# A streaming-encoder trunk on one Trainium2 core: the steps of a Strassen-like feed-forward put in one fixed order, engine by engine

## The chip, the core and the metric

The kernel runs on one core of one Trainium2 chip. The core has TensorE for matrix products (PE in the profile, PEld its loads of the stationary operand), VectorE (DVE), ScalarE (ACT), GpSimd (POOL) and SyncE, whose queue (SP) issues the DMAs here. Each engine works through its own instructions in the order in which they stand in the program, and waits on semaphores for the others.

The metric is the time of the program on the device, in microseconds (us), lower is better. It is taken over several runs; one further run is profiled, and all times of single instructions come from that one.

## What is computed

Two layers act on x of shape (1, 512, 1024) in float32. Layer 0 mixes by pooling, layer 1 by chunked attention with 16 heads; each is followed by a gated feed-forward of width 2816. The change touches the feed-forward of both layers and nothing else:

```python
def conv_ffn(h, w_gate, w_val, conv_w, conv_b, w_out):
    S = h.shape[1]
    a = h @ w_gate
    ap = jnp.pad(a, ((0, 0), (CONV_W - 1, 0), (0, 0)))
    a = ap[:, 0:S] * conv_w[0] + ap[:, 1:S + 1] * conv_w[1] + ap[:, 2:S + 2] * conv_w[2] + conv_b
    return (jax.nn.silu(a) * (h @ w_val)) @ w_out

def reference(x, ...):
    for i in range(DEPTH):
        h = rmsnorm(x, mix_norm[i])
        ...
        h = rmsnorm(x, ffn_norm[i])
        x = x + conv_ffn(h, ffn_w_gate[i], ffn_w_val[i], ffn_conv_w[i], ffn_conv_b[i], ffn_w_out[i])
    return x
```

## The kernel before

**Tiles.** The width of 2816 is cut into 22 tiles of 128, called f = 0 to 21. The frames stand along the free dimension (512), channels along the partitions. Every float32 operand of a product is held as two parts: a high part (the value rounded to the format that TensorE takes) made by ScalarE with a copy, and a low part (value minus high part) made by VectorE. A product is high x high, high x low and low x high, all summed in one bank of PSUM.

**Kinds of tiles** (`KIND`, L53). Tiles 0 and 1 are made early, 2 to 4 in the plain way, tile 5 by `apart`, tiles 6 to 21 by `strassen` (L581). Tiles 8 to 21 are "wide": a product's high and low moving parts go through TensorE as one matmul of 512 columns.

**One Strassen tile.** Gate and value weights of the tile are treated as a 2 x 2 block problem that takes seven products instead of eight. In the order of TensorE they are b11, b21, t2, t3, t1, b22, t4. A wide product is four matmuls of 512 columns (L601) and four of 256 (L603). The products b11, t2, t1 and b22 add up in one bank (`st_m`), b21 has its own (`st_b`), t3 and t4 share a third (`st_t`). The steps around them, with the short names used below (a number in brackets is the line):

- s1 to s4 (L631, L632, L638, L639), VectorE: sums and differences of the raw weights, into the tiles `sb` and `sa`; s2 needs s1, s4 needs s2.
- h1, h2, h3 (L406, ScalarE, 1024 wide) and l1, l2, l3 (L407, VectorE): high and low parts of the gate weights, of `sa` and of `sb`. h4, l4 (L99, L100, 512 wide): those of the value weights' last block. b11 and b21 need h1 and l1, t2 and t3 need h2 and l2, t1 and b22 need h3 and l3, t4 needs h4 and l4.
- a1 (L607, ScalarE) copies b11 out of PSUM, v1 t2, x1 t1, a3 (L669) b22. Since these four products share a bank, t2 waits for a1, t1 for v1, and b22 for x1.
- a2 and x2 (L613, VectorE) add b21 and t3; a5, v2, x3 (L619) and a4 (L671) fold the two halves of a bank together; v3 and v4 (L679) add t4.
- c0 (L418, ScalarE), c1 and c2 (L421, VectorE) are the convolution, c3 (L422, ScalarE) the SiLU, c4 (L672, VectorE) the product with the value, c5 (L99, ScalarE) and c6 (L100, VectorE) the high and low part of the result, which the output product reads.

**Places.** `tour` (L707) interleaves neighbouring tiles: while tile f is made, tile f-1 (o) is finished and tile f+1 (n) is begun. Each round of a tile has seven places, 0 to 6; on TensorE they are b11 of f, b22 of o, b21 of f, t4 of o, t2 of f, t3 of f, t1 of f. A table of letters says whose next steps are issued at a place:

```python
for k, who in enumerate(("of", "fo", "of", "fon", "of", "fon", "nf")):
```

**Output products.** The 22 tiles go to the output in four groups (`OUT`, L55: 5, 6, 6 and 5 tiles). While group g+1 is made, the output of group g (`output`, L684) is worked off behind the places: after each product some three or four matmuls of it follow, so that they are spread over the group. For each of the eight output tiles d there is one load of weights `wo_r` (its buffer is single), a high part `ow_h` (ScalarE) and a low part `ow_l` (VectorE), 15 or 18 matmuls, and an addition to X (L703, VectorE) that waits for the last of them. The spreading begins some places after the group before is complete (L58, used at L759):

```python
WAIT, HOLD = 2, 3
```

**What sets the order.** TensorE's order is written out by hand everywhere in the feed-forward. From tile 8 on (`ORDERED`, L54) VectorE's and ScalarE's are too: they run what is issued at a place in the order of the code. For earlier tiles a scheduler orders these two. SyncE's queue holds the loads in the order in which they are asked for, each waiting until its buffer is free.

Of the kernel before, what the change touches and what calls it, by code (L numbers as in the profile page):

```python
# [17 lines left out]
F32 = mybir.dt.float32  # L18
F32R = mybir.dt.float32r
# [4 lines left out]
P = 128  # L24
S = 512
# [44 lines left out]
def trunk(ctx: ExitStack, tc: tile.TileContext, xt, xT, cols, band, edge, poolw, gv, wout, wqk, wv, wo, rel, out):  # L70
# [307 lines left out]
    def ffn(l, first, pool, acc, summed=None):  # L378
# [35 lines left out]
        def hidden(f, a, finish):  # L414

            cw = [col[:, C_CW[l] + 4 * f + j:C_CW[l] + 4 * f + j + 1] for j in range(4)]
            c = g_tile(f"c{f}")
            nc.scalar.activation(c, a, AF.Identity, scale=cw[2], bias=cw[3])  # L418
            yield
            for j in range(1, 3):  # L420
                nc.vector.scalar_tensor_tensor(c[:, j:], a[:, :S - j], cw[2 - j], c[:, j:], op0=OP.mult, op1=OP.add)  # L421
# [159 lines left out]
        def strassen(f):  # L581

            wide = f in WIDE
            g, v = (raw_tile(f"gv{l}_{f}_{i}", gv[l, f, i]) for i in range(2))
            yield

# [3 lines left out]
            def product(o, hl, z, name, first):  # L590


# [9 lines left out]
                for i, c in enumerate(cs):  # L602
                    nc.tensor.matmul(o[:, 0], lo[:, c], B[i, name][:, 0], start=False, stop=i == 3, **how)  # L603

            def copy(x, o):
# [14 lines left out]

            def flat(o):
                return o.rearrange("p c n -> p (c n)")


            *w1, lo = parts(g, 1024, f"g1_{f}", later=True)
            yield
            lo()
            yield
            sa, sb = (sum_tile(f"s{x}{f}") for x in "ab")
            a11, a12, a21, a22, s2, s3, s1, s4 = (x[:, z * S:(z + 1) * S] for x in (g, v, sa, sb) for z in range(2))  # L630
            nc.vector.tensor_add(s1, a21, a22)  # L631
            nc.vector.tensor_sub(s2, s1, a11)  # L632
            main, side = bank("S", "m"), bank("P", "b")
            product(main, w1, 0, "b11", True)
            yield
            a = pool.tile([P, S], F32, name=f"a{f}", tag="a", bufs=2)
            copy(a, main)
            nc.vector.tensor_sub(s3, a11, a21)  # L638
            nc.vector.tensor_sub(s4, a12, s2)  # L639
            *w2, lo = parts(sa, 1024, f"g2_{f}", later=True)  # L640
            yield
            lo()
            product(side, w1, 1, "b21", True)
            yield
            add(a, side)
            fold(a[:, :HALF], a)
            *w3, lo = parts(sb, 1024, f"g3_{f}", later=True)
            yield
            lo()
            product(main, w2, 0, "t2", False)  # L650
            yield
# [5 lines left out]
            yield  # L657
            w4 = [tmp.tile([P, S], F32R, name=f"g4_{f}_{c}", tag="g", bufs=6) for c in "hl"]
            split(a22, *w4)
            product(main, w3, 0, "t1", False)  # L660
            yield
            x = g_tile(f"w{f}") if wide else val[:, HALF:]
            copy(x, main)
            add(x, side)
            fold(val[:, HALF:], x)
            yield
            product(main, w3, 1, "b22", False)
            yield
            nc.scalar.activation(a[:, HALF:], main[:, 0], AF.Copy)  # L669
            if wide:  # L670
                nc.vector.tensor_add(a[:, HALF:], a[:, HALF:], main[:, 1])  # L671
            gate = hidden(f, a, lambda c: nc.vector.tensor_mul(c, val, c))  # L672
            next(gate)
            yield
            next(gate)
            product(side, w4, 0, "t4", False)
            yield
            for c in range(2 if wide else 1):
                nc.vector.tensor_add(val[:, :HALF], val[:, :HALF], side[:, c])  # L679
            yield  # L680
            run(gate)
            yield

        def output(g):  # L684
# [22 lines left out]
        def tour():  # L707

            for f in range(NF):
                if KIND[f] == "p":  # L710
                    yield from plain(f)
                elif KIND[f] == "s" and KIND[f - 1] == "p":
                    old, new = None, strassen(f + 1)
                    for j, _ in enumerate(apart(f)):
                        if j in (3, 5, 6):
                            next(new)
                        yield
                elif KIND[f] == "s":
                    now, new = new, strassen(f + 1) if f + 1 < NF else None
                    for k, who in enumerate(("of", "fo", "of", "fon", "of", "fon", "nf")):  # L720
                        if f == ORDERED and k == 0:
                            order.enter_context(tc.manual_schedule(engines={ET.DVE, ET.Activation}))
                        for x in who:
                            if step := {"o": old, "f": now, "n": new}[x]:
                                next(step)
                        if old or k not in (1, 3):
                            yield
                    old = now
            for k in range(6):
                next(old)  # L730
                if k in (1, 3):
                    yield
            order.close()

        with tc.manual_schedule(engines={mybir.EngineType.PE}):
# [13 lines left out]
            for g, (b, m) in enumerate(OUT):  # L749
# [3 lines left out]
                for at in range(1, points + 1):  # L753
# [350 lines left out]
```

## Time and profile before

| what | value |
|---|---|
| time, 3 runs | median 1029.67 us (1029.55 to 1029.67) |
| the profiled run's own time | 1029.36 us |
| its span, first to last instruction | 1027.6 us |
| granted TensorE clock, mean over the span | 0.993 |
| DMA | 102.82 MB, mean 100 GB/s |

The rows of the profile read so: start and length in us, engine, line, operation, output <- inputs, shape, count; in square brackets how long the engine stood idle just before and which instruction released it. Groups of instructions show the busy time, the mean length in ns, and the idle time before them with its releaser. A busy TensorE is not TensorE at its peak, since a matmul's length overlaps with the next one's: 0.39 us long, they start every 0.23 us.

### The profile page before, as it was taken

The numbers are of one execution on the slowest core, as the hardware profiler recorded it, in microseconds if no ns is written. First come the engines' busy times: TensorE is split into PE (matmuls) and PEld (weight loads), VectorE is DVE, ScalarE is ACT, GpSimd is POOL, SyncE is SP. The second block draws the span as 40 slices with busy tenths as digits, with TensorE's granted clock in tenths as the row PEclk, the third lists the DMA queues.
The fourth block names the chain that finished last, engine by engine and source line by source line (L and its number), as shares of the span: only waits on it lengthen the run. The fifth ranks groups of instructions, "written<-read, shape, count | busy, mean of one in ns | idle before, by whom it ended". The sixth has DMA issues, their size and how long they took to land.

```text
span 1027.6 us, 13793 instructions
## 1 busy us (share of the span) xinstructions
PE 983.9 (96%) x5038; PEld 818.3 (80%) x5038; DVE 823.2 (80%) x1452; ACT 570.7 (56%) x990; POOL 103.2 (10%) x90
## 2 busy tenths in 40 slices
PE   9999999899999899999999999999999899988998
PEld 8788987787877688888888787888987677776776
DVE  8999888888888855452677888999888888888853
ACT  7665555454554445344898987565554545454431
POOL 2200000000000004103535441000000000000000
PEclk9999999999989999999999999999999999999999
DMA  8322323232323224323343242322332233222223
GB/s 324 97 82 84 104 88 97 82 102 89 98 73 113 57 67 146 103 86 108 115 124 98 84 122 73 112 92 88 103 105 78 92 92 93 92 92 93 63 75 114
DMA packets 37427, 102.82 MB, mean 100 GB/s; under 512 B 4432, under 2 KB 7904, under 8 KB 37360
## 3 DMA queue, kind: packets, MB, share of 16 engines
q1 hardware_dynamic: 37296, 101.90, 31.3%
q8 instruction: 40, 0.66, 0.2%
q14 instruction: 27, 0.22, 0.1%
q0 software_dynamic: 32, 0.04, 0.0%
q10 hardware_dynamic: 32, 0.00, 0.0%
HBM read 95.60 MB, written 2.14 MB: 95 GB/s over the span
## 4 chain that ended last, share of the span: by engine, by line
PE 49%; DVE 37%; ACT 10%; issue 3%; DMA 0%; DVEq 0%; ACTq 0%
DVE g_l L407 8%; ACT g_h L406 5%; DVE c L421 4%; PE out L121 4%; PE out L122 4%; PE out L120 4%; DVE ow_l L100 3%; PE gv L121 3%; PE qk L121 3%; PE qk L120 3%; PE qk L122 3%; PE gv L122 3%; PE gv L120 3%; DVE v L679 2%; DVE v L619 2%
## 5 line engine op out<-in xcount | busy, mean ns | idle before, releaser
L601 PE MATMUL st_m<-two,g_h 128*128 128x512 f32 x224 | 74.7, 415 | 20.5 <-ACT g_h L406 14.9
L121 PE MATMUL out<-one,ow_h 128*128 128x512 f32 x224 | 88.3, 394 | 0.0
L122 PE MATMUL out<-one,ow_l 128*128 128x512 f32 x224 | 88.3, 394 | 0.0
L120 PE MATMUL out<-one,ow_h 128*128 128x512 f32 x224 | 88.2, 394 | 0.0
L99 ACT ACTIVATE ow_h<-wo_r 128x640 fp32r<-128x640 f32 (+1 forms) x64 | 50.2, 784 | 43.8 <-PE out L121 35.7
L406 ACT ACTIVATE g_h<-sa 128x1024 fp32r<-128x1024 f32 x32 | 34.0, 1061 | 72.1 <-DVE sa L638 65.2
L601 PEld LDWEIGHTS st_m<-two,g_h 128*128 128x128 f32 x224 | 40.4, 192 | 40.4 <-ACT g_h L406 25.3
L703 DVE TENSOR_TENSOR X<-out,X 128x512 f32<-128x512 f32 (+1 forms) x65 | 44.0, 678 | 35.6 <-PE out L122 35.6
L601 PE MATMUL st_m<-h,g_h 128*128 128x512 f32 x224 | 70.3, 395 | 0.0
L603 PEld LDWEIGHTS st_m<-two,g_l 128*128 128x128 f32 x224 | 40.1, 190 | 34.8 <-DVE g_l L407 28.2
L100 DVE TENSOR_TENSOR ow_l<-wo_r,ow_h 128x640 fp32r<-128x640 f32 (+1 forms) x64 | 56.7, 885 | 14.0 <-ACT ow_h L99 14.0
L603 PE MATMUL st_m<-two,g_l 128*128 128x256 f32 x224 | 48.2, 298 | 14.8 <-DVE g_l L407 13.7
L422 ACT ACTIVATE c<-c 128x512 f32<-128x512 f32 x44 | 27.6, 630 | 58.8 <-DVE c L421 58.7
L421 DVE SCALAR_TENSOR_TENSOR c<-a,col,c 128x511 f32<-128x511 f32 (+1 forms) x76 | 56.6, 747 | 2.8 <-ACT c L418 1.8
L122 PE MATMUL qk<-wqk_h,two 128*128 128x512 f32 x128 | 51.4, 402 | 0.0
L120 PE MATMUL qk<-wqk_h,two 128*128 128x512 f32 x128 | 50.8, 409 | 0.0
L601 PEld LDWEIGHTS st_m<-h,g_h 128*128 128x128 f32 x224 | 42.9, 192 | 9.9
L121 PE MATMUL qk<-wqk_l,two 128*128 128x512 f32 x128 | 50.8, 397 | 0.0
L122 PEld LDWEIGHTS out<-one,ow_l 128*128 128x128 f32 x224 | 42.6, 190 | 6.5
L120 PEld LDWEIGHTS out<-one,ow_h 128*128 128x128 f32 x224 | 42.5, 190 | 6.2
L99 ACT ACTIVATE one<-c 128x512 fp32r<-128x512 f32 x28 | 17.6, 629 | 53.0 <-DVE c L672 51.8
L121 PEld LDWEIGHTS out<-one,ow_h 128*128 128x128 f32 x224 | 42.6, 190 | 5.3
(375 smaller groups left out, 2998.3 us busy)
## 6 DMA issues: line engine op xcount, KB each, us to landing
gv_r<-gv SPq DMA_DIRECT2D x86, 512.0 KB, 3.4
wo_r<-wout SPq DMA_DIRECT2D x32, 384.0 KB, 3.1
wo_r<-wout SPq DMA_DIRECT2D x32, 320.0 KB, 2.9
wqk_r<-wqk SPq DMA_DIRECT2D x16, 512.0 KB, 3.5
wv_r<-wv SPq DMA_DIRECT2D x8, 512.0 KB, 3.4
wo_r<-wo SPq DMA_DIRECT2D x8, 512.0 KB, 3.4
xt<-xt SPq DMA_DIRECT2D x4, 512.0 KB, 5.2
X<-xT SPq DMA_DIRECT2D x8, 256.0 KB, 7.6
```

What stands on the lines that cost most here:

```text
L99: nc.scalar.activation(hi, raw, AF.Copy)
L100: return (eng or nc.vector).tensor_sub(lo, raw, hi.bitcast(F32))
L120: yield nc.tensor.matmul(o, sh, mh, start=first, stop=False, **how)
L121: yield nc.tensor.matmul(o, sh, ml, start=False, stop=False, **how)
L122: yield nc.tensor.matmul(o, sl, mh, start=False, stop=last, **how)
L406: nc.scalar.activation(hi[:, :n], raw[:, :n], AF.Copy)
L407: return hi, lo, lambda: nc.vector.tensor_sub(lo[:, :n], raw[:, :n], hi[:, :n].bitcast(F32))
L421: nc.vector.scalar_tensor_tensor(c[:, j:], a[:, :S - j], cw[2 - j], c[:, j:], op0=OP.mult, op1=OP.add)
L422: silu = nc.scalar.activation(c, c, AF.Silu)
L601: nc.tensor.matmul(o, hi[:, c], B[i, name], start=first and i == 0, stop=False, **how)
L603: nc.tensor.matmul(o[:, 0], lo[:, c], B[i, name][:, 0], start=False, stop=i == 3, **how)
L703: nc.vector.tensor_add(X[d][:, fs], o[:, fs], X[d][:, fs])
```

## The change

`strassen` no longer issues its steps in code order between yields: each step becomes a function with a name, and a new table `PLACES` says for each of the seven places which steps of which tile are issued there, in which order (q is tile f-2, o f-1, f itself, n f+1). `tour` reads the table. In `hidden` (c0 to c6) every VectorE and ScalarE step is now a step of its own. In `output`, the low part of the weights of output tile d+1 is made after the second pair of products of d instead of together with the high part, and that of d = 0 when the first output matmul of the group is issued. `WAIT` becomes a number for each group, so that the outputs of groups 1 and 2 begin two places later than before.

```diff
+PLACES = ("o.x1 q.c5 f.s2 o.x2 f.s3 o.x3 f.b11", "f.a1 f.h2 f.s4 o.l4 q.c6 n.load o.b22", "o.a3 f.h3 f.l2 o.a4 f.b21", "o.c0 f.a2 f.l3 f.a5 o.t4",
+          "n.h1 f.h4 o.c1 o.v3 o.c2 o.v4 f.t2", "f.v1 o.c3 n.l1 f.v2 f.t3", "n.s1 o.c4 f.t1")
+
 OUT = ((0, 5), (5, 6), (11, 6), (17, 5))
 GM = 6
-WAIT, HOLD = 2, 3
+WAIT, HOLD = (0, 2, 4, 4), 3
...
             for j in range(1, 3):
                 nc.vector.scalar_tensor_tensor(c[:, j:], a[:, :S - j], cw[2 - j], c[:, j:], op0=OP.mult, op1=OP.add)
+                yield
...
             finish(c)
-            split(c, *slot[f])
+            yield
+            nc.scalar.activation(slot[f][0], c, AF.Copy)
+            yield
+            nc.vector.tensor_sub(slot[f][1], c, slot[f][0].bitcast(F32))
...
-            val = g_tile(f"v{f}")
-            copy(val, main)
-            fold(val[:, :HALF], val)
-            side = bank("S", "t")
-            product(side, w2, 1, "t3", True)
-            yield
...
+            @step
+            def v1():
+                nonlocal val
+                val = g_tile(f"v{f}")
+                copy(val, main)
+
+            @step
+            def v2():
+                fold(val[:, :HALF], val)
+
+            @step
+            def t3():
+                nonlocal side
+                side = bank("S", "t")
+                product(side, w2[:2], 1, "t3", True)
...
-                w.append(parts(raw_tile(f"wo{l}_{g}_{d}", wout[l, d, :, b * P:(b + m) * P], n, g + 1 < len(OUT)), n, f"ow{l}_{g}_{d}", True))
+                w.append(parts(raw_tile(f"wo{l}_{g}_{d}", wout[l, d, :, b * P:(b + m) * P], n, g + 1 < len(OUT)), n, f"ow{l}_{g}_{d}", True, True))
 
             load(0)
             yield
+            w[0][2]()
             for d in range(KD):
                 if d + 1 < KD:
                     load(d + 1)
                 o = psum("Q", f"out{l}_{g}_{d}")
                 for i in range(m):
+                    if i == 2 and d + 1 < KD:
+                        w[d + 1][2]()
...
+            def place(f, k):
+
+                for word in PLACES[k].split():
+                    x, name = word.split(".")
+                    step = steps_of(f + "qofn".index(x) - 2).get(name)
+                    if step:
+                        step()
...
-                    if at > WAIT:
-                        due = (todo - hold) * (at - WAIT) // (points - WAIT)
+                    wait = WAIT[g]
+                    if at > wait:
+                        due = (todo - hold) * (at - wait) // (points - wait)
```

The order of instructions moves as follows. On ScalarE, from the end of tile 10's round into tile 11's, the kernel before has this (g1 to g4 are the weights of the products, with the tile's number behind; `_h` and `_l` are high and low parts; `one6` and `one14` take the high and low part of tile 9's result):

```order
L669 ACTIVATE a9_1523<-st0_9_m_1510 128x256
L418 ACTIVATE c9_1687<-a9_1523,col_107 128x512
L406 ACTIVATE g3_10_h_1703<-sb10_1643 128x1024
L422 ACTIVATE c9_1687<-c9_1687 128x512
L607 ACTIVATE v10_1737<-st0_10_m_1646 128x512
L99 ACTIVATE one6_86<-c9_1687 128x512
L406 ACTIVATE g1_11_h_1752<-gv0_11_0_r_1717 128x1024
L99 ACTIVATE g4_10_h_1759<-gv0_10_1_r_1583 128x512
L607 ACTIVATE w10_1776<-st0_10_m_1646 128x512
```

At the same place of ScalarE the changed kernel has:

```order
L763 ACTIVATE a9_1521<-st0_9_m_1509 128x256
L409 ACTIVATE g3_10_h_1688<-sb10_1624 128x1024
L421 ACTIVATE c9_1706<-a9_1521,col_107 128x512
L409 ACTIVATE g1_11_h_1722<-gv0_11_0_r_1672 128x1024
L717 ACTIVATE g4_10_h_1725<-gv0_10_1_r_1531 128x512
L619 ACTIVATE v10_1742<-st0_10_m_1645 128x512
L426 ACTIVATE c9_1706<-c9_1706 128x512
L619 ACTIVATE w10_1776<-st0_10_m_1645 128x512
L433 ACTIVATE one6_86<-c9_1706 128x512
```

The next tile's high part h1 (`g1_11_h`) stood behind the SiLU c3, the copy v1 and the high part c5 of tile 9; now it stands ahead of all three, and c5 comes behind x1 (`w10`).

On VectorE at the same stretch of the program, before:

```order
L672 TENSOR_TENSOR c9_1687<-v9_1601,c9_1687 128x512
L100 TENSOR_TENSOR one14_94<-c9_1687,one6_86 128x512
L407 TENSOR_TENSOR g1_11_l_1753<-gv0_11_0_r_1717,g1_11_h_1752 128x1024
L100 TENSOR_TENSOR g4_10_l_1760<-gv0_10_1_r_1583,g4_10_h_1759 128x512
L703 TENSOR_TENSOR X6_78<-out0_0_6_1665,X6_78 128x512
L613 TENSOR_TENSOR w10_1776<-w10_1776,st0_10_t_1740 128x512
L619 TENSOR_TENSOR v10_1737<-w10_1776 128x256
L631 TENSOR_TENSOR sb11_1781<-gv0_11_1_r_1719 128x512
L632 TENSOR_TENSOR sa11_1780<-sb11_1781,gv0_11_0_r_1717 128x512
L638 TENSOR_TENSOR sa11_1780<-gv0_11_0_r_1717,gv0_11_1_r_1719 128x512
L639 TENSOR_TENSOR sb11_1781<-gv0_11_0_r_1717,sa11_1780 128x512
```

And in the changed kernel:

```order
L410 TENSOR_TENSOR g1_11_l_1723<-gv0_11_0_r_1672,g1_11_h_1722 128x1024
L631 TENSOR_TENSOR v10_1742<-v10_1742 128x256
L651 TENSOR_TENSOR sb11_1760<-gv0_11_1_r_1674 128x512
L786 TENSOR_TENSOR c9_1706<-v9_1606,c9_1706 128x512
L817 TENSOR_TENSOR X6_78<-out0_0_6_1662,X6_78 128x512
L655 TENSOR_TENSOR sa11_1759<-sb11_1760,gv0_11_0_r_1672 128x512
L625 TENSOR_TENSOR w10_1776<-w10_1776,st0_10_t_1747 128x512
L659 TENSOR_TENSOR sa11_1759<-gv0_11_0_r_1672,gv0_11_1_r_1674 128x512
L631 TENSOR_TENSOR v10_1742<-w10_1776 128x256
L675 TENSOR_TENSOR sb11_1760<-gv0_11_0_r_1672,sa11_1759 128x512
L721 TENSOR_TENSOR g4_10_l_1726<-gv0_10_1_r_1531,g4_10_h_1725 128x512
L435 TENSOR_TENSOR one14_94<-c9_1706,one6_86 128x512
```

The low part l1 (`g1_11_l`) now comes ahead of c4 and c6 of tile 9, and the pairs s1-s2 and x2-x3, which stood next to each other, have another step between them.

Where the outputs of group 1 begin, in tile 11's and 12's rounds, VectorE before has the low part of their first weights (`ow0_1_0_l`) right behind the last addition of the group before:

```order
L703 TENSOR_TENSOR X7_79<-out0_0_7_1772,X7_79 128x512
L100 TENSOR_TENSOR ow0_1_0_l_1858<-wo0_1_0_r_1855,ow0_1_0_h_1857 128x768
L679 TENSOR_TENSOR v10_1737<-v10_1737,st0_10_t_1740 128x256 x2
L407 TENSOR_TENSOR g3_11_l_1834<-sb11_1781,g3_11_h_1833 128x1024
L619 TENSOR_TENSOR v11_1872<-v11_1872 128x256
```

In the changed kernel 15 steps stand between the two; these are the last of them and what follows:

```order
L631 TENSOR_TENSOR v11_1876<-w11_1902 128x256
L675 TENSOR_TENSOR sb12_1891<-gv0_12_0_r_1803,sa12_1890 128x512
L721 TENSOR_TENSOR g4_11_l_1862<-gv0_11_1_r_1674,g4_11_h_1861 128x512
L435 TENSOR_TENSOR one15_95<-c10_1836,one7_87 128x512
L410 TENSOR_TENSOR ow0_1_0_l_1856<-wo0_1_0_r_1853,ow0_1_0_h_1855 128x768
L410 TENSOR_TENSOR g2_12_l_1921<-sa12_1890,g2_12_h_1920 128x1024
L768 TENSOR_TENSOR a11_1795<-a11_1795,st0_11_m_1783 128x256
L410 TENSOR_TENSOR ow0_1_1_l_1942<-wo0_1_1_r_1939,ow0_1_1_h_1941 128x768
```

On TensorE the first three output matmuls of that group stood behind t1 of tile 11; in the changed kernel they stand behind its b22, with b11 of tile 12 and that b22 ahead of them:

```order
L612 MATMUL st0_11_m_1783<-h5_472,g3_11_l_1820 128x256
L123 MATMUL out0_1_0_1944<-one2_82,ow0_1_0_h_1855 128x512
L124 MATMUL out0_1_0_1944<-one10_90,ow0_1_0_h_1855 128x512
L125 MATMUL out0_1_0_1944<-one2_82,ow0_1_0_l_1856 128x512
L610 MATMUL st0_12_b_1954<-two1_97,g1_12_h_1858 128x512
```

The third of them is the first to read the low part. Apart from these shifts of output matmuls, the order of TensorE is the same.

More of the change, by code (lines that the diff above doesn't have):

```diff
@@ L633, in strassen @@
[L633 to L645, printed above, removed]
@@ L660, in strassen @@
[L660 to L672, printed above, removed]
@@ L673, in strassen, with load, h1 @@
[L673 to L682, printed above, removed]
+            @step
+            def load():
+                nonlocal raws
+                raws = [raw_tile(f"gv{l}_{f}_{i}", gv[l, f, i]) for i in range(2)]
+            @step
+            def h1():
+                nonlocal w1
+                w1 = parts(raws[0], 1024, f"g1_{f}", later=True)
@@ new lines, in l2, with h3, l3, b21 @@
+            @step
+            def l2():
+                w2[2]()
+            @step
+            def h3():
+                nonlocal w3
+                w3 = parts(sb, 1024, f"g3_{f}", later=True)
+            @step
+            def l3():
+                w3[2]()
+            @step
+            def b21():
+                nonlocal side
+                side = bank("P", "b")
+                product(side, w1[:2], 1, "b21", True)
+            @step
+            def a2():
+                add(a, side)
@@ L707, in tour, with steps_of @@
         def tour():
[L709 to L713, printed above, removed]
+            tiles = {}
+            def steps_of(f):
+                if f not in tiles:
+                    tiles[f] = strassen(f) if f < NF and KIND[f - 1] == "s" else {}
+                return tiles[f]
+            def place(f, k):
[4 more added lines that the diff above has]
+                        step()
@@ L717, in tour @@
                         yield
[L718 to L733, printed above, removed]
+                    continue
+                for k in range(7):
+                    if (f, k) == (ORDERED, 0):
+                        order.enter_context(tc.manual_schedule(engines={ET.DVE, ET.Activation}))
+                    place(f, k)
+                    if steps_of(f - 1 if k in (1, 3) else f):
+                        yield
+                    if (f, k) == (NF, 3):
+                        order.close()
```

127 lines of the change are left out of this document (105 added, 22 removed).

## The prediction

> **What bounds the kernel now.** I read the busy line of the page first, then a table by stretches, then the costliest groups, the waits, and last the timeline of two places.
>
> ```profile
> PE 983.9 (96%) x5038; PEld 818.3 (80%) x5038; DVE 823.2 (80%) x1452; ACT 570.7 (56%) x990; POOL 103.2 (10%) x90
> 60.00:139.53 79.53, 79.44 (x477) 70.88 (x476) 74.46 (x119) 47.47 (x72) 0.00 (x0) 1.00 0.31 98
> 139.53:363.98 224.45, 208.85 (x1031) 169.66 (x1030) 193.13 (x298) 108.43 (x162) 0.00 (x0) 0.97 0.29 89
> 759.93:984.05 224.12, 204.49 (x1032) 165.29 (x1030) 193.07 (x298) 108.23 (x162) 0.00 (x0) 1.00 0.29 89
> ```
>
> TensorE bounds the program as a whole, and it has idle time in only two long stretches. They run, in layer 0 and in layer 1, from b11 of tile 9 to the moment when the outputs of group 2 stand alone. The columns are the stretch's length, then busy time of PE, PEld, DVE, ACT and POOL, then the granted clock. Just ahead, from 60 to 139.53, TensorE is busy for 79.44 of 79.53 us, so there is nothing to win there.
>
> Since matmuls overlap, idle time understates the loss. I take TensorE's free pace from an undisturbed piece, tile 8, and count the work in the stretch by two further rows, those of L601 (four for each product) and of the output matmuls:
>
> ```profile
> 129.29 0.62 PE L601 MATMUL st_b<-two,g_h 128*128 128x512 f32 x2
> ...
> 130.68 0.40 PE L120 MATMUL out<-u3h,ow_h 128*128 128x512 f32 x1
> ...
> 131.38 0.28 PE L120 MATMUL st_t<-two,g_h 128*128 128x256 f32 x1
> 139.53:363.98 224.45, 104.59 (x372) 70.16 (x371) 0.97 0.29 89
> 139.53:363.98 224.45, 83.14 (x287) 49.33 (x287) 10.94 (x16) 0.97 0.29 89
> ```
>
> A product takes 130.68 - 129.29 = 1.39 us, three output matmuls 131.38 - 130.68 = 0.70, so 0.233 each. The stretch holds 372 / 4 = 93 products and 287 output matmuls: 93 x 1.39 + 287 x 0.233 = 196.1 us. Layer 0 needs 28.3 us more than that, layer 1 28.0. **These 56.3 us are all that the change can win on TensorE.**
>
> Who is waited for, by the costliest groups and the list of waits:
>
> ```profile
> L601 PE MATMUL st_m<-two,g_h 128*128 128x512 f32 x224 | 74.7, 415 | 20.5 <-ACT g_h L406 14.9
> L603 PE MATMUL st_m<-two,g_l 128*128 128x256 f32 x224 | 48.2, 298 | 14.8 <-DVE g_l L407 13.7
> ACT one L99 <- DVE c L672: 51.8, 22, 3.4
> ```
>
> And how it comes about, at b11 of tile 13:
>
> ```profile
> 203.70 0.68 DVE L672 TENSOR_TENSOR c<-v,c 128x512 f32<-128x512 f32 x1
> ...
> 204.42 0.63 ACT L99 ACTIVATE u0h<-c 128x512 fp32r<-128x512 f32 x1 [2.41 <-DVE c L672]
> 204.95 1.04 ACT L406 ACTIVATE g_h<-gv_r 128x1024 fp32r<-128x1024 f32 x1
> 206.03 1.22 DVE L407 TENSOR_TENSOR g_l<-gv_r,g_h 128x1024 fp32r<-128x1024 f32 x1 [0.26 <-ACT g_h L406]
> 206.05 0.73 PE L601 MATMUL st_m<-two,g_h 128*128 128x512 f32 x2 [0.69 <-ACT g_h L406]
> ```
>
> ScalarE stands 2.41 us for c4 of an older tile, only then makes c5, and h1 is queued behind it. h1 needs nothing but loaded weights. TensorE and VectorE then wait for h1 and l1. It is order that costs time here, not work: VectorE is busy for 193 of 224 us, ScalarE for 108.
>
> **The change part by part.**
>
> *Order.* No arithmetic is added or taken away. h1 moves from place 5 to 4, l1 from 6 to 5, s1 to place 6, the load of the next weights from place 3 to 1 (two places earlier in SyncE's queue). Now b11 at place 0 finds h1 made two places earlier and l1 one place and a half. The same count for the others: l2 place 2 for t2 at 4, l3 place 3 for t1 at 6, l4 place 1 for t4 at 3, x2 place 0 for t4 at 3. The short distances are ScalarE's: v1 (place 5) for t1 (6), and x1 (0) for b22 (1).
>
> Does VectorE keep up? Its steps, start to start:
>
> ```profile
> 200.76 1.22 DVE L407 TENSOR_TENSOR g_l<-sb,g_h 128x1024 fp32r<-128x1024 f32 x1
> 201.90 0.68 DVE L703 TENSOR_TENSOR X<-out,X 128x512 f32<-128x512 f32 x1
> 202.50 0.95 DVE L100 TENSOR_TENSOR ow_l<-wo_r,ow_h 128x768 fp32r<-128x768 f32 x1
> 203.36 0.42 DVE L619 TENSOR_TENSOR v<-v 128x256 f32<-128x256 f32 x1
> ...
> 208.83 0.68 DVE L631 TENSOR_TENSOR sb<-gv_r 128x512 f32<-128x512 f32 x1
> 209.55 0.69 DVE L632 TENSOR_TENSOR sa<-sb,gv_r 128x512 f32<-128x512 f32 x1
> 210.16 0.68 DVE L638 TENSOR_TENSOR sa<-gv_r,gv_r 128x512 f32<-128x512 f32 x1
> ...
> 216.23 1.53 DVE L421 SCALAR_TENSOR_TENSOR c<-a,col,c 128x511 f32<-128x511 f32 x2
> 217.68 0.87 DVE L679 TENSOR_TENSOR v<-v,st_t 128x256 f32<-128x256 f32 x2
> 218.47 1.22 DVE L407 TENSOR_TENSOR g_l<-sb,g_h 128x1024 fp32r<-128x1024 f32 x1
> ```
>
> s2 reads s1 and starts 0.72 us after it; s3 does not read s2 and starts after 0.61. So a step that reads its predecessor costs 0.11 us more. An independent step of 512 takes 0.61, one of 1024 takes 1.14 (200.76 to 201.90), of 256 0.34 (203.36 to 203.70), 768 0.86. c1 and c2 together take 1.45, so 1.34 apart; v3 and v4 0.79, so 0.68 apart. A tile then costs 8 x 0.61 (s1 to s4, l4, x2, a2, c4) + 0.61 (c6) + 3 x 1.14 + 4 x 0.34 (a4, a5, v2, x3) + 1.34 + 0.68 = 12.3 us, and 0.55 more with the five pairs of before next to each other. Each output tile adds 0.60 + 0.86.
>
> With three output matmuls to a place a tile lasts at least 7 x (1.39 + 0.70) = 14.6 us on TensorE and takes at most 12.3 + 21/15 x 1.46 = 14.3 on VectorE; with four, 16.2 against 12.3 + 28/18 x 1.46 = 14.6. So VectorE keeps up, barely in the first kind. Walking once through the places, with its waits for a2 (b21's end), x2 and the additions to X, I find it at most 1.5 us into the next place, while l1 may be 3 us late before b11 stands. **In the steady tiles I count no wait of TensorE at all.** Bounds: none, and, if VectorE keeps the idle time that it has now, the second rival.
>
> [...]
>
> *Start of groups 1 and 2.* Here the change makes a wait. Take t = 0 at the start of t2 of tile 11 (place 4). TensorE has t2, t3, t1, b11, b22 without outputs between them, 5 x 1.39 = 6.95, then two output matmuls; the third, at 7.42, reads `ow_l` of d = 0. On VectorE that step stands behind everything of places 4 to 6, 0 and 1, and all of it behind the last addition to X of the group before, which TensorE's last output matmul releases:
>
> ```profile
> 368.07 0.39 PE L120 MATMUL out<-u0h,ow_h 128*128 128x512 f32 x1
> ...
> 368.27 0.69 DVE L703 TENSOR_TENSOR X<-out,X 128x512 f32<-128x512 f32 x1 [0.35 <-PE out L122]
> ```
>
> An addition starts about 0.20 us after the next matmul has started. So VectorE: 0.20 + 0.60 (X) + 1.34 (c1, c2) + 0.68 (v3, v4) + 1.14 (l1) + 2 x 0.34 (v2, x3) + 8 x 0.61 (s1, c4, s2, x2, s3, s4, l4, c6) = 9.52, and `ow_l` itself is 0.95 long: 10.47. **TensorE stands 10.47 - 7.42 = 3.05 us at each of the four starts** (two groups, two layers), 12.2 in all. If VectorE comes a microsecond late it is 4; below 2.8 it cannot fall, since X holds the whole queue. Before, the same spot costs this:
>
> ```profile
> 183.96 0.73 PE L601 MATMUL st_m<-two,g_h 128*128 128x512 f32 x2 [1.10 <-ACT v L607]
> 186.39 0.50 PE L603 MATMUL st_m<-two,g_l 128*128 128x256 f32 x2 [1.23 <-DVE g_l L407]
> 180.00:200.00 20.00, 17.18 (x83) 13.68 (x82) 17.13 (x28) 8.97 (x14) 0.00 (x0) 0.91 0.28 93
> 800.00:820.00 20.00, 16.49 (x84) 13.03 (x83) 17.12 (x27) 9.38 (x14) 0.00 (x0) 1.00 0.29 94
> ```
>
> After these two stalls the granted clock was 0.91 over 20 us, a loss of 1.8 us of clock; after the same stalls in layer 1 it stayed at 1.00. Before, this loss cost next to nothing (stretches of 224.45 and 224.12), since TensorE waited for others anyway. After the change TensorE is the bound, and one stall of 3 us is longer than any here. I take 1.2 us for each start, since part of the slow clock falls into the stall: 4.8, with bounds of 0 and 4 x 1.8 = 7.2.
>
> [...]
>
> *Later output weights.* The low part now comes two places behind the high part, so the single buffer of `wo_r` is free later. It lands in
>
> ```profile
> wo_r<-wout SPq DMA_DIRECT2D x32, 384.0 KB, 3.1
> ```
>
> 3.1 us. An output tile of 15 matmuls lasts five places, 10.4 us; the low part is done by 4.2 + 1.0, the transfer by 8.6 with SyncE's issue, and ScalarE asks for it at 10.4: 1.8 us to spare. At a group's start there is none: the second load waits for the late `ow_l`, lands near 14, and ScalarE stands before its high part with a3 and h3 queued behind it. l3 is then done near 17.7, TensorE asks for it near 20 in both groups; but in group 2, with three output matmuls to a place, v1 comes about 0.3 us late. Two layers: 0.6.
>
> *The end of tile 21* has no next b11 between t1 and b22, only three output matmuls, 0.70 us. x1 needs about 0.3 for t1's end to reach it and 0.58 to run, and its result must reach TensorE: 0.3 us, twice, 0.6.
>
> **Sum,** against the profiled run: span 1027.6 - 56.3 + 12.2 + 4.8 + 0.6 + 0.6 = 989.5. The run itself was 1029.36, 1.8 more than its span: 991.3. The median of the runs is 0.3 above that run: **991.6 us**.
>
> **The rivals.**
>
> - *The clock stays up* at the group starts: 991.6 - 4.8 = 986.8. For it: layer 1's row. Against it: layer 0's.
> - *VectorE becomes the bound.* Its waits for a2, x2, a4 and X do not shrink with TensorE's, and it stands idle as long as now: 224.45 - 193.13 = 31.3 us a stretch. Only the spacing is won, 13 tiles x 0.55 = 7.2 a stretch: 1029.7 - 14.3 = 1015.4. For it: 14.3 against 14.6 is tight. Against it: now VectorE waits for ScalarE, and that chain is what the new order cuts.
> [...]
> - *The wait only moves:* in-order queues meet each other at another place and nothing is won: 1029.
> - *Slower: ScalarE stands behind a late `wo_r`.* If VectorE is over 1.8 us late at the low parts, every load in the places with three output matmuls, some 13 a layer, holds ScalarE, and a3, h3 and c0 behind it, for a landing of 3.1 us: 26 x 3.1 = 81 against 56 won, 1029.7 + 25 = 1054. Against it: VectorE has waits of its own to catch up in.
> - *Everything goes,* the group starts too: 975.
>
> **How the numbers follow.** Chances: forecast 0.58 (984 to 1000), clock up 0.12, VectorE bound 0.15, spacing worthless 0.03, wait moves 0.04, slower 0.04, everything goes 0.04. The time is the forecast's, 991.6. From 982 to 1016 the range takes in the first four, 0.88 by these chances, less what lies at their edges: about 0.8. Faster by over 0.2% (2 us, about what a measurement of this kernel can tell) takes all but two cases: 0.92; same 0.04; slower 0.04.
>
> **What would show it.** Right: the two stretches fall to about 205 us; the idle time of L601's and L603's matmuls on `st_m` is gone but for the two starts in each layer, where the first output matmul that reads `ow_l` (now on L125) stands some 3 us for VectorE; ScalarE no longer waits for c4 before h1; s2 starts 0.6 us after its predecessor. The clock's slices show whether a start costs a slow stretch. Wrong: matmuls of steady tiles that wait for l1, v1 or x1; ScalarE standing for a landing in every output tile; VectorE busy throughout while TensorE waits.

## The result, and the profile after

| kernel | median | runs | ratio to before, 95% interval |
|---|---|---|---|
| before | 1029.67 us | 1029.55 to 1029.90, 4 runs | |
| changed | 991.78 us | 989.22 to 993.14, 4 runs | 0.9629, 0.9608 to 0.9650 |

The profiled run of the changed kernel took 991.02 us with a span of 989.2. The busy line of its page:

```profile
PE 968.9 (98%) x5038; PEld 822.3 (83%) x5038; DVE 805.4 (81%) x1452; ACT 573.8 (58%) x990; POOL 103.2 (10%) x90
```

The two stretches that the prediction rests on, in the same columns (length, then busy time of PE, PEld, DVE, ACT and POOL, granted clock, DMA share, GB/s):

```profile
139.80:343.34 203.54, 197.96 (x1031) 168.59 (x1030) 183.32 (x296) 109.88 (x163) 0.00 (x0) 0.99 0.30 100
739.27:945.74 206.47, 200.88 (x1032) 170.94 (x1031) 184.07 (x296) 110.53 (x163) 0.00 (x0) 0.98 0.30 98
```

Both stretches again run from b11 of tile 9 to the outputs that stand alone. They shrank by 20.9 and 17.7 us, 38.6 together; the span shrank by 38.4. So all of the gain lies in them. VectorE's busy time there is 9 to 10 us less: where a step does not read the one before it, the two overlap a little (`ow_l` at 186.31 starts 0.61 us after c6 at 185.70, which is 0.68 long). About half of this comes from keeping the dependent pairs apart (188.25 us in layer 0 with the pairs adjacent again, against 183.32 here; the run is below); where the other half comes from was not traced.

From the groups (busy time, mean ns of one, idle time before them) and from the list of waits, the rows that answer to those of before:

```profile
L610 PE MATMUL st_m<-two,g_h 128*128 128x512 f32 x224 | 70.0, 394 | 0.0
L612 PE MATMUL st_m<-two,g_l 128*128 128x256 f32 x224 | 44.4, 280 | 0.0
```

```profile
ACT one L433 <- DVE c L786: 6.7, 8, 1.8
PE out L125 <- DVE ow_l L410: 11.2, 4, 2.8
```

The products no longer wait for their weights at all (20.5 and 14.8 us before). TensorE has one kind of wait left in these tiles, four times 2.8 us, for the low part of the output weights. At b11 of tile 13, where before h1 stood behind c5 and c5 behind c4, ScalarE and VectorE now show:

```profile
193.87 1.05 ACT L409 ACTIVATE g_h<-gv_r 128x1024 fp32r<-128x1024 f32 x1
...
197.61 1.22 DVE L410 TENSOR_TENSOR g_l<-gv_r,g_h 128x1024 fp32r<-128x1024 f32 x1
...
199.06 0.62 PE L610 MATMUL st_m<-two,g_h 128*128 128x512 f32 x2
199.69 0.68 DVE L786 TENSOR_TENSOR c<-v,c 128x512 f32<-128x512 f32 x1
...
200.40 0.63 ACT L433 ACTIVATE u0h<-c 128x512 fp32r<-128x512 f32 x1 [1.10 <-DVE c L786]
```

h1 is ready 4.1 us ahead of b11, and c4 and c5 run behind it; c5 still stands 1.10 us for c4, but nothing that TensorE needs soon is queued behind it.

The start of group 1 in layer 0, TensorE and the VectorE steps around it:

```profile
177.10 0.69 DVE L817 TENSOR_TENSOR X<-out,X 128x512 f32<-128x512 f32 x1 [0.63 <-PE out L125]
...
184.12 0.40 PE L124 MATMUL out<-one,ow_h 128*128 128x512 f32 x1
...
185.70 0.68 DVE L435 TENSOR_TENSOR one<-c,one 128x512 fp32r<-128x512 f32 x1
186.31 0.95 DVE L410 TENSOR_TENSOR ow_l<-wo_r,ow_h 128x768 fp32r<-128x768 f32 x1
...
187.31 0.50 PE L125 MATMUL out<-one,ow_l 128*128 128x512 f32 x1 [2.79 <-DVE ow_l L410]
```

From the last addition of the group before (177.10) VectorE goes through 15 steps without a pause before it reaches `ow_l` at 186.31; c6 at 185.70 is the last of them. TensorE starts the third output matmul 3.19 us after the second instead of 0.23, a stall of 2.96.

### The profile page after: what moved, and what is told of

It reads as the page before. It is cut to its first block, busy times and chain, and to the rows that moved or that the text cites. A ratio compares the mean times of both kernels' runs of the same rounds, so it can differ in the third digit from the quotient of the medians.

```text
span 989.2 us, 13813 instructions
## 1 busy us (share of the span) xinstructions
PE 968.9 (98%) x5038; PEld 822.3 (83%) x5038; DVE 805.4 (81%) x1452; ACT 573.8 (58%) x990; POOL 103.2 (10%) x90
## 4 chain that ended last, share of the span: by engine, by line
PE 91%; DVE 5%; ACT 2%; issue 1%; DMA 0%; DVEq 0%; ACTq 0%
PE st_m L610 9%; PE out L125 8%; PE out L123 8%; PE out L124 8%; PE st_t L610 5%; PE st_m L612 5%; PE gv L124 4%; PE gv L123 4%; PE gv L125 4%; PE qk L124 3%; PE qk L123 3%; PE qk L125 3%; PE st_b L610 3%; PE st_t L612 2%; PE tp L1059 2%; PE oo L1071 2%
## 5 line engine op out<-in xcount | busy, mean ns | idle before, releaser
L610 PE MATMUL st_m<-two,g_h 128*128 128x512 f32 x224 | 70.0, 394 | 0.0
L619 ACT ACTIVATE w<-st_m 128x512 f32<-128x512 f32 x28 | 16.7, 597 | 54.2 <-PE st_m L612 54.2
L1047 DVE CUSTOM_DVE_ANT_0 sb<-sc,B 128x128 f32<-128x128 f32 (+1 forms) x64 | 31.1, 486 | 18.8 <-PE sc L1044 18.1
L612 PE MATMUL st_m<-h,g_l 128*128 128x256 f32 x224 | 45.1, 283 | 0.0
L148 POOL TENSOR_TENSOR n_acc<-n_acc,n_sq 128x512 f32<-128x512 f32 x7 | 9.6, 1366 | 336.1 <-ACT n_sq L146 336.1
```

What stands on the lines that cost most here:

```text
L610: nc.tensor.matmul(o, hi[:, c], B[i, name], start=first and i == 0, stop=False, **how)
L1047: nc.vector.tensor_tensor_reduce(out=s_[:, :n], in0=sc[:, :n], in1=BT[h % 2][:, :n][:, ::-1], scale=1.0, scalar=3e38, op0=OP.add, op1=OP.m ...
```

## The experiments

In the text below, a tile's *loss* is what TensorE's starts, matmul by matmul, lie beyond the free pace (0.2313 us for 512 columns, 0.1175 for 256, the pace that the kernel of the first experiment keeps throughout). It is worked out from all matmul rows of a trace, and it counts slow clock as well as waits. For each kernel that was run, the text that stands first is what was expected of it before it ran. All times are medians of four runs unless said otherwise; the kernel before took 1029.1 to 1030.0 us beside them.

### The low part of the first output weights, earlier

```diff
             load(0)
             yield
             w[0][2]()
+            yield
...
+                    if g and at == 3:
+                        next(queue[0])
                     wait = WAIT[g]
```

> Only the low part ow_l of output tile 0 of groups 1 and 2 is issued earlier, right behind place 6 instead of behind place 1. Theory (the forecast's step on the group starts): VectorE reaches it at 0.20 + 0.60 + 1.34 + 0.68 + 1.14 + 0.34 + 2 x 0.61 and ends it 0.95 later, at 6.5 us; the third output matmul asks at 7.42, so all four stalls (3.06, 3.32, 3.17, 3.32 in the changed kernel, 12.9 us) go, and with them the half-speed clock behind them (5.1 us in the profiled run): 991.8 - 12.9 - 5.1 = 973.8, and a mean clock of 1.00 in the windows of the starts. Rival (the stall hides other waits): matmuls that wait for l4, l2 or v1 of the first places take its room, 986 or more. Rival on the clock (the slow stretches do not come from the stalls): 973.8 + 5.1 = 979.

Measured 972.78 us (972.71 to 973.07), ratio 0.9446 (0.9432 to 0.9460). The two stretches of this kernel:

```profile
139.40:335.42 196.02, 196.02 (x1031) 167.71 (x1030) 183.43 (x296) 110.41 (x163) 0.00 (x0) 1.00 0.32 104
731.40:927.42 196.02, 196.02 (x1031) 167.71 (x1030) 183.50 (x296) 111.26 (x163) 0.00 (x0) 1.00 0.32 104
```

TensorE is busy for the whole of each, at full clock, and no tile from 9 to 20 loses more than 0.02 us. The stall and the slow clock are gone together, and no other wait took their room. 196.02 is what the stretch's work takes (the prediction's 196.1). This kernel is 19.0 us faster than the changed one.

### The low parts beside their high parts again

```diff
-                w.append(parts(raw_tile(f"wo{l}_{g}_{d}", wout[l, d, :, b * P:(b + m) * P], n, g + 1 < len(OUT)), n, f"ow{l}_{g}_{d}", True, True))
+                w.append(parts(raw_tile(f"wo{l}_{g}_{d}", wout[l, d, :, b * P:(b + m) * P], n, g + 1 < len(OUT)), n, f"ow{l}_{g}_{d}", True))
...
-            w[0][2]()
...
-                    if i == 2 and d + 1 < KD:
-                        w[d + 1][2]()
```

> The changed kernel without its later low parts: every ow_l stands right behind its high part again, so the one of a group's first output tile stands right behind the last addition to X. Theory (the later low part of the other output tiles is worth little, and that of output tile 0 is the whole loss of the group starts): no stall at the starts, and VectorE stands up to 0.3 us for each high part: 973 to 977. Rival (the later low parts are needed, since VectorE otherwise stands for ScalarE at every output tile): 983 or more.

Measured 972.88 us (972.61 to 972.93), ratio 0.9448 (0.9432 to 0.9464), the same as the run above; its stretch in layer 0:

```profile
139.52:335.55 196.03, 196.03 (x1031) 167.72 (x1030) 183.53 (x296) 110.13 (x163) 0.00 (x0) 1.00 0.32 102
```

So in this order the later low parts win nothing, and that of output tile 0 costs the changed kernel 19 us. The later start of the outputs (`WAIT`) was not tried by itself.

### Half of the stall

The edit of the first experiment with `at == 4`.

> As the run with the earlier low part, but one place later, behind place 0: three steps of VectorE less in front of it than in the changed kernel (s4, l4, c6, 3 x 0.60 = 1.81), so each of the four stalls is 2.96 - 1.81 = 1.15 us start to start instead of 2.96. [...] Rival (any stall of this kind brings a slow stretch, as the stalls of 1.1 and 1.2 us seemed to do before): 1.2 more each, 982, and runs 2 us apart or more.

Measured 978.55 us (978.33 to 978.93), ratio 0.9504 (0.9490 to 0.9518); four stalls of 1.15 on top of 972.8 come to 977.4. Its span and mean clock, and from the list of waits TensorE's in these tiles:

```profile
core 0: 976.8 us, clock 1.000
```

```profile
PE out L125 <- DVE ow_l L410: 3.9, 4, 1.0
...
PE st_m L610 <- ACT v L619: 0.6, 1, 0.6
```

Four stalls, 1.25 us each beyond the free pace, bring no slow stretch (mean clock 1.000), and the runs agree within 0.6 us; those of the changed kernel are 3.9 apart. The remaining microsecond is the last row: at the start of group 2 in layer 0, v1 stood behind a late landing of `wo_r`, and that tile lost 0.9.

### The order of before, and its pairs

This kernel has the order of before, written into the changed kernel's table (the tile ahead of the first Strassen tile no longer makes its s1 early either):

```diff
+PLACES = ("o.x1 o.x2 o.x3 f.s1 f.s2 f.b11", "f.a1 f.s3 f.s4 f.h2 o.b22", "o.a3 o.a4 o.c0 f.l2 f.b21",
+          "f.a2 f.a5 f.h3 o.c1 o.c2 o.c3 n.load o.t4", "o.v3 o.v4 f.l3 f.t2",
+          "f.v1 f.v2 o.c4 o.c5 o.c6 n.h1 f.t3", "n.l1 f.h4 f.l4 f.t1")
```

> The changed kernel with the order of steps of before put into its table (dependent pairs next to each other, h1 behind c5, l1 at place 6); the later low parts of the output weights and the later outputs stay. Theory (order is what gains): TensorE waits for h1 and l1 in every wide tile again, 28 us a layer lost less what the stalls hid, and the time is 1015 to 1035. Rival (the later low parts and the later start of the outputs gain): 1000 or less.

Measured 1035.03 us, ratio 1.0050 (1.0035 to 1.0065). The order is worth all of the gain and more: with the order of before, the later low parts and outputs alone cost 5 us, since their stalls at the group starts come on top (four waits of TensorE for `ow_l`, 9.8 us in its trace).

Then the pairs alone, in both directions. In the order of before, kept apart:

```diff
-"o.x1 o.x2 o.x3 f.s1 f.s2 f.b11"             "f.a2 f.a5 f.h3 o.c1 o.c2 o.c3 n.load o.t4"  "o.v3 o.v4 f.l3 f.t2"
+"o.x1 o.x2 f.s1 o.x3 f.s2 f.b11"             "f.a2 o.c1 f.h3 f.a5 o.c2 o.c3 n.load o.t4"  "o.v3 f.l3 o.v4 f.t2"
```

> The order of before in the changed kernel (1035.0), with its five dependent pairs of VectorE kept apart by a neighbour of the same place; ScalarE's order stays. Theory (in that order VectorE is not what sets the pace, so spacing is worth little): 1030 to 1035. Rival (spacing alone wins 0.55 us in 13 tiles of two layers): 1021.

Measured 1018.74 us, ratio 0.9894 (0.9879 to 0.9908): 16.3 us less than 1035.03. My theory fell here, the rival's 14.3 was nearly right. The stretch in layer 0, the pairs adjacent and then apart:

```profile
139.83:366.30 226.47, 207.06 (x1031) 166.69 (x1030) 192.78 (x300) 108.24 (x162) 0.00 (x0) 0.99 0.29 90
```

```profile
139.80:359.04 219.24, 205.65 (x1031) 168.24 (x1030) 186.83 (x300) 108.26 (x162) 0.00 (x0) 0.98 0.29 93
```

7.2 us less is 13 tiles x 0.55, to a tenth (layer 1 gains 8.8). VectorE stands still for 33.7 us in the one and 32.4 in the other (length less busy time), and waits for ScalarE make up nearly all of it; the largest two, of the kernel with the pairs apart:

```profile
DVE a L768 <- ACT a L763: 20.1, 13, 5.9
DVE one L435 <- ACT one L433: 6.3, 9, 0.7
```

Of the 7.2 us, about 6 are VectorE's busy time (192.78 to 186.83). So in the old order VectorE's own steps lie on the path, though TensorE's waits name ScalarE. Keeping a pair apart also moves its neighbour forward (c1 now stands ahead of a5); this run does not separate the two.

And in the changed kernel, next to each other again:

```diff
-"o.x1 q.c5 f.s2 o.x2 f.s3 o.x3 f.b11"  "o.c0 f.a2 f.l3 f.a5 o.t4"  "n.h1 f.h4 o.c1 o.v3 o.c2 o.v4 f.t2"  "n.s1 o.c4 f.t1"
+"o.x1 q.c5 f.s2 o.x2 o.x3 f.s3 f.b11"  "o.c0 f.a2 f.a5 f.l3 o.t4"  "n.h1 f.h4 o.c1 o.c2 o.v3 o.v4 f.t2"  "o.c4 n.s1 f.t1"
```

> The changed kernel, ScalarE's order as it is, with the five dependent pairs of VectorE next to each other again (s1 s2, x2 x3, a2 a5, c1 c2, v3 v4). Theory (a step that reads its predecessor costs 0.11 us more, and tiles with three output matmuls to a place have VectorE at its limit): 14.85 us a tile against 14.6, 0.25 x 12 tiles, and 0.44 more at each of four starts: 991.8 + 4.8 = 996.6; a start's stall is 3.5 instead of 3.06 to 3.32, and a dependent step stands 0.72 behind its predecessor. Rival (spacing is worth nothing): 991.8, no step's distance changed. Rival (spacing is much of the gain): over 1003.

Measured 993.23 us (992.18 to 994.99), ratio 0.9646 (0.9631 to 0.9660): 1.4 more than the changed kernel, which the intervals don't tell apart. The trace shows a difference, though. VectorE's a2 and a5 (L625, L631), TensorE's waits, and the stretch in layer 0:

```profile
160.92 0.68 DVE L625 TENSOR_TENSOR a<-a,st_b 128x512 f32<-128x512 f32 x1
161.64 0.43 DVE L631 TENSOR_TENSOR a<-a 128x256 f32<-128x256 f32 x1
```

```profile
PE out L125 <- DVE ow_l L410: 13.2, 4, 3.3
...
PE st_m L610 <- ACT v L619: 1.3, 2, 0.8
```

```profile
139.49:344.69 205.20, 197.33 (x1031) 167.28 (x1030) 188.25 (x297) 109.92 (x163) 0.00 (x0) 1.00 0.30 99
```

A dependent step stands 0.72 behind its predecessor, and the four waits at the starts are 13.2 us instead of 11.2, 0.5 each (0.44 expected). The steady tiles lose 1.0 us in layer 0 and nothing in layer 1, not 3; VectorE stands still for 17.0 us of this stretch, against 20.2 in the changed kernel.

### h1 behind c5 again, and h1 alone

In the changed kernel, c4 and c5 back at place 5 with h1 behind them, l1 at place 6:

```diff
-"o.x1 q.c5 f.s2 ..."  "f.a1 f.h2 f.s4 o.l4 q.c6 ..."  "n.h1 f.h4 o.c1 ..."  "f.v1 o.c3 n.l1 f.v2 f.t3"                "n.s1 o.c4 f.t1"
+"o.x1 f.s2 ..."       "f.a1 f.h2 f.s4 o.l4 ..."       "f.h4 o.c1 ..."       "f.v1 o.c3 o.c4 o.c5 n.h1 f.v2 f.t3"      "n.l1 o.c6 n.s1 f.t1"
```

> The changed kernel with one chain put back: c4 and c5 at place 5, and h1 of the next tile behind c5 on ScalarE, l1 at place 6, as before; pairs stay apart. Theory (h1's place behind c4 is what costs time before): b11 of each wide tile waits for h1 or l1 again, half a microsecond to one in 26 tiles: 1005 to 1018, and waits on the matmuls into st_m released by g_h or g_l. Rival (the gain is VectorE's spacing or its other order): 992 to 996.

Measured 1016.00 us, ratio 0.9868 (0.9851 to 0.9884): 24.2 of the 37.9 us won are lost again. TensorE's waits:

```profile
PE st_m L610 <- ACT g_h L409: 17.3, 11, 2.9
PE out L125 <- DVE ow_l L410: 9.2, 4, 2.9
```

The wait for h1 is back. In the four tiles that have four output matmuls to a place (13 to 16) little is lost (0.5 us in layer 0, 1.6 in layer 1); the loss sits where the places are shorter, and around the starts.

The converse, in the order of before:

```diff
-"f.a1 f.s3 f.s4 f.h2 o.b22"         "f.a2 f.a5 f.h3 o.c1 o.c2 o.c3 n.load o.t4"  "o.v3 o.v4 f.l3 f.t2"       "f.v1 f.v2 o.c4 o.c5 o.c6 n.h1 f.t3"  "n.l1 f.h4 f.l4 f.t1"
+"f.a1 f.s3 f.s4 f.h2 n.load o.b22"  "f.a2 f.a5 f.h3 o.c1 o.c2 o.c3 o.t4"         "n.h1 o.v3 o.v4 f.l3 f.t2"  "f.v1 f.v2 n.l1 o.c4 o.c5 o.c6 f.t3"  "f.h4 f.l4 f.t1"
```

> The order of before in the changed kernel (1035.0), with only h1 of the next tile moved to the head of place 4, its l1 ahead of c4 at place 5, and the load of its weights to place 1, as the changed order has them. Theory (h1 behind c4 and c5 is most of the loss): the waits of the first product of a tile for h1 and l1 go, and some 20 to 25 us are won: 1010 to 1015. Rival (the wait only moves to v1, x1 or l2, and all moves are needed together): 1025 or more.

Measured 1035.79 us, ratio 1.0060 (1.0045 to 1.0075): nothing won, the rival was right. TensorE's waits, and ScalarE around v1 of tile 13:

```profile
PE st_m L610 <- ACT v L619: 27.6, 22, 2.6
```

```profile
219.88 0.63 ACT L426 ACTIVATE c<-c 128x512 f32<-128x512 f32 x1 [1.93 <-DVE c L424]
220.42 0.83 ACT L409 ACTIVATE ow_h<-wo_r 128x768 fp32r<-128x768 f32 x1
221.16 1.04 ACT L409 ACTIVATE g_h<-gv_r 128x1024 fp32r<-128x1024 f32 x1
222.10 0.57 ACT L619 ACTIVATE v<-st_m 128x512 f32<-128x512 f32 x1
```

h1 is early, but it and v1 now stand behind the SiLU c3, which stands 1.93 us for c2; t1 waits for v1 instead of b11 for h1.

### From the order of before to the new one, step by step

Three kernels go on from the last one, each with one more edit. First c6 and l4 go to place 0, so that they no longer stand right behind c5 and h4, whose results they need:

```diff
-"o.x1 o.x2 o.x3 f.s1 f.s2 f.b11"            "f.v1 f.v2 n.l1 o.c4 o.c5 o.c6 f.t3"  "f.h4 f.l4 f.t1"
+"o.x1 q.c6 o.l4 o.x2 o.x3 f.s1 f.s2 f.b11"  "f.v1 f.v2 n.l1 o.c4 o.c5 f.t3"       "f.h4 f.t1"
```

> The order of before with h1 moved (1035.8, where VectorE is busy 192.8 us of a stretch of 227.1 and waits for ScalarE in nearly all the rest), with c6 and l4 one place later, at place 0. The SiLU c3 and c5 stay where ScalarE stands for c2 and c4. Theory formed after the run that moved h1 alone (in this order VectorE's queue together with its waits for ScalarE sets the pace): c6's waits for c5, 14 x 0.70 = 9.8 us a stretch, go, and 1035.8 - 19.6 = 1016. Rival (ScalarE's queue sets the pace by standing for c2 and c4, 27.6 and 28 us a stretch): those waits are left as they are, 1030 or more.

Then l2 between a3 and a4:

```diff
-"o.a3 o.a4 o.c0 f.l2 f.b21"
+"o.a3 f.l2 o.a4 o.c0 f.b21"
```

> As the run before it, and l2 stands between a3 and a4, so that VectorE no longer asks for a3 at once. Theory (VectorE's queue with its waits): 11 waits of 0.8 us in the steady tiles of a stretch go, 8.8 each: 1016 - 17.6 = 998. Rival (ScalarE's queue): no gain, 1030 or more.

Then three pairs apart:

```diff
-"o.x1 q.c6 o.l4 o.x2 o.x3 f.s1 f.s2 f.b11"  "n.h1 o.v3 o.v4 f.l3 f.t2"
+"o.x1 q.c6 f.s1 o.x2 f.s2 o.x3 o.l4 f.b11"  "n.h1 o.v3 f.l3 o.v4 f.t2"
```

> As the run before it, with s1 s2, x2 x3 and v3 v4 kept apart (a2 a5 and c1 c2 stay next to each other). Theory (VectorE's queue with its waits): 0.33 us less in 13 tiles of a stretch, but TensorE's own work and the stalls of the group starts (203.5 and 206.5 us in the changed kernel) are reached before that: 991 to 995, as the changed kernel, though c3 and c5 still stand behind c2 and c4 in ScalarE's queue. Rival (ScalarE's queue): 1020 or more.

Measured: 1028.34 us (10 runs; ratio 0.9980, 0.9970 to 0.9989), 1015.81 (0.9863, 0.9848 to 0.9878) and 1011.28 (0.9819, 0.9804 to 0.9834). That is 7.5, 12.5 and 4.5 us won, where the theory of the one queue wanted 19.6, 17.6 and 3 to 7, and its rival nothing. Both fell. After the third, TensorE still waits for v1 (the whole program), and ScalarE for c2 (layer 0's stretch):

```profile
PE st_m L610 <- ACT v L619: 13.1, 14, 1.9
```

```profile
ACT c L426 <- DVE c L424: 12.8, 13, 1.7
```

Last, the convolution one place later:

```diff
-"o.x1 q.c6 f.s1 ..."  "f.a1 f.s3 f.s4 f.h2 n.load o.b22"       "f.a2 f.a5 f.h3 o.c1 o.c2 o.c3 o.t4"  "n.h1 o.v3 f.l3 o.v4 f.t2"            "f.v1 f.v2 n.l1 o.c4 o.c5 f.t3"  "f.h4 f.t1"
+"o.x1 q.c5 f.s1 ..."  "f.a1 f.s3 f.s4 f.h2 q.c6 n.load o.b22"  "f.a2 f.a5 f.h3 o.t4"                 "n.h1 o.v3 f.l3 o.v4 o.c1 o.c2 f.t2"  "f.v1 o.c3 f.v2 n.l1 f.t3"       "f.h4 o.c4 f.t1"
```

> As the run before it (1011.3, where TensorE waits 13.1 us for v1, which stands behind h1, and h1 behind the SiLU c3, which stands for c2), with the convolution chain one place later: c1 and c2 at place 4, c3 behind v1 at place 5, c4 at place 6, c5 at place 0, c6 at place 1. Theory (no one queue sets the pace: every step that asks for a result of the other engine from its own place costs its share, and these are the last of them): the steady tiles lose nothing, only the stalls of the group starts are left, 991 to 995. Rival (the places of s1, h4, l3, or the pairs a2 a5 and c1 c2, are needed too): 1000 or more. Rival (ScalarE's standing behind c2 is harmless): 1008 to 1013.

Measured 997.45 us (995.47 to 999.81), ratio 0.9685 (0.9668 to 0.9701): 13.8 won. The same two views:

```profile
PE out L125 <- DVE ow_l L410: 13.6, 4, 3.4
PE st_m L612 <- DVE g_l L410: 1.5, 4, 0.4
```

```profile
ACT c L426 <- DVE c L424: 16.5, 13, 2.0
```

The steady tiles lose nothing, as expected; of the tiles from 9 to 20 only 12 and 18, with the starts, lose more than 0.02 us. That the time lies 2.5 us above the expected range is the starts: each waits 3.4 us for `ow_l` and 0.4 for l1, and slow clock behind them (mean 0.987 over the span, 0.993 in the changed kernel) brings the loss of the two stretches to 27.1 us, against 18.2 in the changed kernel. And ScalarE stands *longer* for c2 than in the kernel before this one (16.5 against 12.8 us), at no cost, since v1 and h1 are now ahead of c3.

## Why the prediction was right, point by point

- **What could be won.** 56.3 us, and two stretches of about 205: they are 203.5 and 206.5. Where no wait is left they are 196.02, against the 196.1 counted.
- **Steady tiles without a wait.** Right: tiles 9 to 11, 13 to 17, 19 and 20 lose 0.01 us or less in both layers.
- **The group starts.** Forecast 3.05 us each, 12.2. The output matmuls there lost 3.06, 3.32, 3.17 and 3.32, 12.9 in all, with part of the slow clock in it. That 15 steps of VectorE ahead of `ow_l` are the cause is shown: with three of them fewer the loss is 1.25, with seven fewer (the first experiment) it is none.
- **The clock term.** Forecast 4.8, 0 to 7.2. The profiled run lost 5.1: nothing behind the first start, 1.08, 1.45 and 2.55 behind the others. It differs from run to run: at mean clocks of 0.996, 0.993, 0.991 and 0.991 the runs took 989.2, 991.0, 993.1 and 992.5 us. The rival in which the clock stays up fell: it was 0.50 for a time behind three of the four starts (last section). That the single starts (0 to 2.55, for a forecast of 1.2 each) add up to nearly the forecast is in part luck, and with it that the median lies within 0.2 us of 991.6: the runs of this kernel are 3.9 us apart.
- **The late `wo_r`.** The chain was right, its price was not. The landing was forecast near 14 us behind t2 of tile 11, and ScalarE got it at 191.20 - 176.90 = 14.3, after a wait of 5.87:

```profile
191.20 0.85 ACT L409 ACTIVATE ow_h<-wo_r 128x768 fp32r<-128x768 f32 x1 [5.87 <-DMA wo_r<-wout]
```

  At group 2, for which the 0.3 us a layer was forecast, it came later, 15.4 and 15.0 behind t2 of tile 17, and yet v1 was not late. Slow clock behind both of these starts (0.50 from 281.82 and from 882.57 on, 1.08 and 2.55 us lost) had moved TensorE back far enough: with the shorter stall (mean clock 1.000 over the span), and with the pairs adjacent (1.00 over layer 0's stretch), the start of group 2 in layer 0 kept full clock, and there v1 was late, which cost 0.9 and 1.0. So a term of the sum fell away because of another one, the slow clock.
- **Tile 21.** Forecast 0.3 us a layer, found 0.27 (0.16 and 0.11 around t1).
- **Spacing.** The step's cost (0.11, from 0.72 against 0.61) was right. Its worth in the new order was mis-sized: 0.25 us in 12 tiles, 3 us, by the expectation of the run with the pairs adjacent, where that run shows 1.0, and VectorE stood still 3.2 us less in that stretch, so it had time to give. The 0.44 for each start, 1.8, became 2.0.
- **The step that did not hold** is the sentence on the cause, that h1 is queued behind c5 and c5 stands for c4, and that this chain is what the new order cuts. Putting it back costs 24 us, so it is necessary to cut it. But cutting it alone won nothing: v1 then stands behind c3 and c2 in its place. The runs show a ring of VectorE and ScalarE with several such places, of which the new order leaves none that TensorE waits for in the steady tiles. How much each of them is worth by itself stays open, and has no single answer: keeping the pairs apart is worth 16.3 us in the order of before, 4.5 in the third of the stepwise kernels (three of the five pairs), and at most some 3 (1.0 + 2.0) in the new order.
- **The rivals.** That VectorE becomes the bound and only the spacing is won (14.3) did not happen in the changed kernel, but describes the old order with its pairs apart (16.3). That everything goes, the starts too (975), is what the first experiment reached (972.8).

## What to carry to other kernels

In an in-order queue, look not at the step that waits but at what is queued behind it: moving one urgent step past a wait wins nothing while another stands ahead of the next urgent step (1035.79 us after 1035.03), and a long wait with nothing urgent behind it is free (the 16.5 us that ScalarE stands for c2 in the last kernel). When such an order frees TensorE, every wait that the old losses covered costs its full length, and it can cost clock as well (here behind three of the four stalls of 2.96 us, behind none of the four of 1.15), so look through the few irregular places (a group's start, its first operands) by hand. A step that is postponed only for the sake of a rule, as the low part here, should show in the trace what that wins.

## What the runs showed of the hardware

**The granted clock behind a stall was not the same each time.** The changed kernel has the same stall at its four group starts, 2.96 us beyond the free pace. TensorE around their ends (columns: length, busy time of TensorE, granted clock, DMA share, GB/s):

```profile
184.00:190.00 6.00, 3.21 (x17) 1.00 0.61 212
282.00:290.00 8.00, 7.72 (x33) 0.80 0.41 151
783.00:792.00 9.00, 6.20 (x25) 0.81 0.46 160
880.00:890.00 10.00, 7.21 (x23) 0.66 0.40 144
```

Behind the first the clock stayed at 1.00. Behind the others it was 0.50, from 281.82 to 285.23, from 786.99 to 790.41 and from 882.57 to 889.39, and two matmuls of 512 columns at 282.88 took 0.85 us from start to start, 0.43 each instead of 0.23. In the kernel before, the same two stalls (1.10 and 1.23 us) were followed by 0.91 over 20 us in layer 0 and by 1.00 in layer 1; in the kernel with the pairs adjacent, TensorE's waits of 3.3 us left layer 0's stretch at 1.00; and four stalls of 1.15 us left the mean of the whole span at 1.000. What decides whether the clock falls was not shown.

**Steps of VectorE.** By the prediction's rows an independent step (s3, 210.16) starts 0.61 us after a predecessor of 512 that is itself 0.69 long, and a dependent one (s2, 209.55) after 0.72, as again in the kernel with the pairs adjacent (160.92 to 161.64). With spacing worth 16.3 us in the order of before (1018.74 against 1035.03) the difference is no small thing.
